# A low-rank update kernel: matrix A read by one transfer of 12 rows in place of three of 4 rows

## The chip, the cores and the metric

The kernel runs on one core of a Trainium2 chip. The metric is the device time of one execution in microseconds (us); lower is better. The core has five engines with an instruction stream each: TensorE (PE in the profile; PEld is its weight load), VectorE (DVE), ScalarE (ACT), GpSimd (POOL) and SyncE (SP). Here SP computes nothing: it only issues transfers, and all of the kernel's transfers go through its one queue. 16 DMA engines carry them out. Engines and transfers are kept in order by semaphores, which the kernel sets and waits for by hand.

## The reference

```python
batch, seq, d_model, r = 16, 512, 768, 16
x: (16, 512, 768) float32, A: (768, 16) float32, B: (16, 768) float32, scale = 0.5
lora = np.matmul(np.matmul(x, A), B)
return (x + scale * lora).astype(np.float32)
```

x has 8192 tokens of 768 values, 25.2 MB in and as much out. A and B are 48 KB each. To every token a correction of rank 16 is added.

## The kernel before, in words

**Tiling.** The tokens are cut into five parts (`PARTS = [9, 7, 16, 16, 16]`, in units of 128 tokens). Inside a part, each of the 128 partitions holds that many consecutive tokens, so a transfer's row in one partition is one long contiguous piece. All of x stays in on-chip memory (`x_sb`), in float32; the last part takes the place of the first two, once these are stored. A unit of 128 tokens is called a tile here; 64 tiles are worked on in 8 groups of 8.

**One group.** ScalarE and GpSimd cast four tiles each to float16 (`narrowed`, line 194, into `xn`). VectorE transposes them in 32 x 32 blocks (`turned`, line 250, into `xt`). TensorE multiplies the transposed tokens with a block-diagonal arrangement of A (`projected`, line 281, weights `w_bd`, result `y_ps`). ScalarE scales the 16 values per token and spreads them on the diagonal blocks of `y_bd` (line 238). TensorE multiplies these with B (`raised`, line 302, weights `y_bd`, moving `b_mm`, result in `lora_ps`). VectorE adds the result to x in place (`summed`, line 255). The store sends x back.

**The transfers, all on SP** (`on_sync`). In this order: load 0 (2 tiles) and load 1 (7 tiles) of x; then SP waits until `a_rows` is cleared and issues the three transfers of A (line 156); it waits until `b_rows` is cleared and issues B (line 160); then loads 2 to 5 (7, 8, 8 and 16 tiles). From there on each issue waits for something: stores 0 and 1 for the additions of the first two groups, load 6 for store 0 to land, load 7 for store 1, stores 2 to 4 for the sums of their parts (store 2 also for the start of the sixth group's product with B). Line 139 issues a load, line 149 a store.

**How A gets into its place.** A is seen as 12 blocks of 64 of its rows (`blocks`, 12 rows of 1024 values, 4 KB each). The first 32 partitions of `a_rows` are cleared by GpSimd (line 199). Transfer c (0, 1, 2) puts blocks 4c to 4c+3 into partitions c, c+4, c+8 and c+12. Each of the three adds 16 to the semaphore `s_a` when it has landed; GpSimd's first cast of x adds 1 to the same semaphore. VectorE waits until it is 49 and then transposes the 32 partitions of `a_rows` into `a_t` (line 243). GpSimd copies the 12 valid columns to float16 in block order (`w_one`, line 214), and then four times into the diagonal places of `w_bd` (line 220), which TensorE needs for its first projection.

**How B gets into its place.** Its 16 rows go into every fourth partition of `b_rows`; GpSimd casts them (line 212), TensorE spreads them over all partitions with a selecting matrix (line 315), and ScalarE copies the result to `b_mm` (line 231).

The order of the start on the other engines: GpSimd clears five tiles (lines 199 to 203), casts the first two tiles of x, casts B, then builds `w_one` and `w_bd`. ScalarE casts the other six tiles of the first group. VectorE transposes A first, then the first group's casts in two halves.

Of the kernel before, what the change touches and what calls it, by code (L numbers as in the profile page):

```python
# [18 lines left out]
SUB = 4  # L19

APART = 4
SETS, SET = 3, 4


@with_exitstack
def kernel(
# [11 lines left out]
    Q = 32  # L41
# [6 lines left out]
    NC = D // 64  # L48
# [6 lines left out]
    def sb(name, shape, dtype):  # L55
        return nc.alloc_sbuf_tensor(name, shape, dtype).ap()
# [10 lines left out]
    a_rows = sb("a_rows", [P, 64 * R], fp32)  # L67
    a_t = sb("a_t", [P, 2, R, Q], fp32)
    w_one = sb("w_one", [Q, NC, 2, R], MM_DT)
# [13 lines left out]
    def sem(name):  # L83
        sems.append(nc.alloc_semaphore(name))
        return sems[-1]
# [10 lines left out]
    def memory(t2, i, s, n):  # L96
        S = PARTS[i]
        return t2[ds(parts[i], S * P), :].rearrange("(p s) d -> p s d", s=S)[:, ds(s, n), :]

    def held(i, s, n):  # L100
        return tiles(where.index((i, s)), n)

    def tiles(t, n):
        return x_all[:, ds(t % ROOM, n), :]
# [7 lines left out]
        i, s = where[t]  # L112
        return next(k for k, ld in enumerate(LOADS) if ld[0] == i and ld[1] <= s < ld[1] + ld[2])

    assert SETS * SET == NC
    s_a, s_b = sem("s_a"), sem("s_b")
    s_ready, s_brows, s_pick = sem("s_ready"), sem("s_brows"), sem("s_pick")
    s_w, s_bh, s_bp, s_bm = sem("s_w"), sem("s_bh"), sem("s_bp"), sem("s_bm")
# [17 lines left out]
    def on_sync(e):  # L136
        def load(k):
            ld = LOADS[k]
            e.dma_start(out=held(*ld), in_=memory(x2, *ld)).then_inc(s_load[k], 16)  # L139

        def summed(k):
            e.wait_ge(s_sum, sorted(set(STORED)).index(STORED[k]) + 1)
            if STORED[k] + 1 < NG:

                e.sem_inc(s_free[PAIRS - 1], 1)

        def store(k, done):
            st = STORES[k]
            e.dma_start(out=memory(out2, *st), in_=held(*st)).then_inc(done, 16)

        load(0)
        load(1)
        e.wait_ge(s_ready, 1)
        blocks = A.rearrange("(c e) r -> c (e r)", e=64)
        for c in range(SETS):
            e.dma_start(
                out=a_rows[c : SET * SET : SET, :], in_=blocks[ds(c * SET, SET), :]
            ).then_inc(s_a, 16)
        e.wait_ge(s_brows, 1)
        e.dma_start(out=b_rows[0 : R * APART : APART, :], in_=B).then_inc(s_b, 16)  # L160
        for k in range(2, len(LOADS) - 2):
            load(k)

        for p in range(2, PAIRS):
            e.sem_inc(s_free[p], 1)
        summed(0)


        e.wait_ge(s_lora, 2 * PAIRS + 2)
        store(0, s_out0)  # L170
        store(1, s_out1)
        e.wait_ge(s_out0, 16)
        load(len(LOADS) - 2)
        e.wait_ge(s_out1, 16)
        load(len(LOADS) - 1)
        for k in range(2, len(STORES)):
            summed(k)
            if k == 2:


                e.wait_ge(s_raise, 6)
            store(k, s_out)
# [3 lines left out]
    def narrowed(e, copy, g, first, n=SUB):  # L186
        t = g * GROUP + first
        for k in dict.fromkeys(load_of(t + k) for k in range(n)):
            if (e, k) not in here:
                here.add((e, k))  # L190
                e.wait_ge(s_load[k], 16)
        if g:
            e.wait_ge(s_taken, g)
        ins = copy(out=xn[:, ds(first, n), :], in_=tiles(t, n))  # L194

        ins.then_inc(s_narrow if g else s_first if first else s_a, 1)

    def on_gpsimd(e):
        e.memset(a_rows[0:Q], 0.0).then_inc(s_ready, 1)  # L199
        e.memset(b_rows, 0.0).then_inc(s_brows, 1)  # L200
        e.memset(pick, 0.0).then_inc(s_pick, 1)
        e.memset(w_bd.rearrange("p c k m -> p (c k m)").bitcast(fp32), 0.0)  # L202
        e.memset(y_bd.rearrange("p s m -> p (s m)").bitcast(fp32), 0.0).then_inc(s_ready, 1)  # L203
        e.wait_ge(s_pick, 1)
        e.affine_select(  # L205
            out=pick, in_=pick, compare_op=mybir.AluOpType.not_equal, fill=1.0, base=0,
            pattern=[[0, NQ], [-APART, Q]], channel_multiplier=1,
        ).then_inc(s_pick, 1)
        narrowed(e, e.tensor_copy, 0, 0, SUB // 2)
        e.wait_ge(s_pick, 2)  # L210
        e.wait_ge(s_b, 16)
        e.tensor_copy(out=b_half, in_=b_rows).then_inc(s_bh, 1)  # L212
        e.wait_ge(s_ready, 3)
        e.tensor_copy(  # L214
            out=w_one.rearrange("i (c e) k r -> i c e (k r)", c=SETS),
            in_=a_t[0:Q].rearrange("i k r (e c) -> i c e (k r)", c=SET)[:, 0:SETS, 0:SET, :],
        ).then_inc(s_w, 1)
        e.wait_ge(s_w, 1)
        for b in range(NQ):
            e.tensor_copy(  # L220
                out=w_bd[ds(b * Q, Q), :, :, ds(b * Q, R)], in_=w_one
            ).then_inc(s_w, 1)
            e.wait_ge(s_w, b + 2)
        for g in range(1, NG):
            narrowed(e, e.tensor_copy, g, SUB)
# [13 lines left out]
            last.then_inc(s_spread, 1)  # L239

    def on_vector(e):
        e.wait_ge(s_a, SETS * 16 + 1)
        e.transpose(  # L243
            out=a_t[0:Q].rearrange("i k r c -> i (k r) c"),
            in_=a_rows[0:Q].rearrange("c (i k r) -> c (k r) i", k=2, r=R),
        ).then_inc(s_ready, 1)

        def turned(first, n):
            ts = [v[:, ds(first, n), :].bitcast(fp32) for v in (xt, xn)]
            return e.transpose(out=ts[0], in_=ts[1])  # L250

        def summed(g, p):
            xs = tiles(g * GROUP + 2 * p, 2)
            e.wait_ge(s_lora, g * PAIRS + p + 1)
            ins = e.tensor_tensor(out=xs, in0=xs, in1=lora[p % 2], op=mybir.AluOpType.add)  # L255
            if p + 1 == PAIRS and g in STORED:
                ins.then_inc(s_sum, 1)
            elif g + 1 < NG or p + 2 < PAIRS:
                ins.then_inc(s_free[p], 1)

        for h in range(2):
            e.wait_ge(s_first, h + 1)
            ins = turned(h * SUB, SUB)
        ins.then_inc(s_turned, 1)
        for g in range(NG):
            if g + 1 < NG:
                e.wait_ge(s_y, g + 1)
                e.wait_ge(s_narrow, 2 * (g + 1))  # L268
                turned(0, GROUP).then_inc(s_turned, 1)
            for p in range(PAIRS):  # L270
                summed(g, p)

    def on_tensor(e):
# [58 lines left out]
        for p in range(PAIRS):  # L332
            raised(p)

    on_sync(nc.sync)
    on_gpsimd(nc.gpsimd)
    on_scalar(nc.scalar)
    on_vector(nc.vector)
    on_tensor(nc.tensor)

# [43 lines left out]
```

## Time and profile before

| what | before |
|---|---|
| time, median of 3 runs | 123.47 us (123.41 to 123.53) |
| time of the profiled execution | 123.43 us |
| its span (first to last instruction) | 121.6 us |
| bytes moved in the span, mean rate | 50.43 MB, 415 GB/s |
| busy time VectorE | 81.7 us (67%) |
| busy time TensorE, its weight load | 49.8 us (41%), 29.2 us (24%) |
| busy time ScalarE, GpSimd | 37.4 us (31%), 28.4 us (23%) |
| three issues of A on SP | 0.58 to 0.76 us each |

The span is what the profiler sees between the first and the last instruction; the measured time has a little more on both sides of it. Times inside the profile count from the start of the span. A timeline line gives start and duration in us, the engine, the source line, the operation, what is written from what is read with the shapes, how often, and in brackets how long the engine sat idle before it and what ended that. SPq is SP's own queue of issues: its durations are those of issuing, not of the transfer.

The trace also has a record of every DMA packet: when it started, how long it took and how many bytes it moved. A packet here is one partition's row of a transfer, or a write of 4 bytes that counts up a semaphore.

### The profile page before, as it was taken

The page shows a single profiled execution, that of the slowest core. Times are in us where ns is not written, and L with a number is a line of the kernel's source. Part 1 is how long each engine was busy: PE and PEld are TensorE (multiplying, and loading weights), DVE is VectorE, ACT ScalarE, POOL GpSimd, SP SyncE. Part 2 cuts the span into 40 slices and gives each one's busy share as a digit, 9 for nine tenths or more (in the row PEclk, how much of TensorE's full clock was granted, in tenths as well). Part 3 has the DMA queues.
Part 4 walks back from the last instruction along what each step waited for, and adds up shares of the span by engine and source line. Part 5 has one row for each costly group of instructions (what it writes and reads, how often), then busy time and mean ns, then how long its engine had stood idle before and what let it go on. Part 6 is the DMA issues. An engine that isn't in the chain of part 4 may idle for free.

```text
span 121.6 us, 884 instructions
## 1 busy us (share of the span) xinstructions
PE 49.8 (41%) x322; PEld 29.2 (24%) x322; DVE 81.7 (67%) x42; ACT 37.4 (31%) x43; POOL 28.4 (23%) x24
## 2 busy tenths in 40 slices
PE   0000209487457547746745734774674320000000
PEld 0000006253223424424423322442442110000000
DVE  0000970599999999999999989999995990000000
ACT  4000967626408312735340093643004000000000
POOL 7730567126009002605300080620000000000000
PEclk9999999999999999999999999999999995555555
DMA  3999999999999897999999999998999899899890
GB/s 63 437 431 457 446 398 469 404 420 469 437 517 420 356 517 336 427 421 410 446 416 436 428 428 485 420 517 372 404 517 404 372 517 404 372 517 404 372 517 0
DMA packets 1928, 50.43 MB, mean 415 GB/s; under 512 B 236, under 2 KB 236, under 8 KB 392
## 3 DMA queue, kind: packets, MB, share of 16 engines
q1 hardware_dynamic: 1928, 50.43, 97.0%
HBM read 25.26 MB, written 25.17 MB: 415 GB/s over the span
## 4 chain that ended last, share of the span: by engine, by line
DVE 33%; DMA 29%; PE 9%; ACT 6%; POOL 2%; issue 2%; SPq 0%; DVEq 0%
DVE x_sb L255 21%; DMA x_sb<-in_x_dram 20%; DVE xt L250 12%; DMA out_dram<-x_sb 9%; PE ps_yt L281 6%; ACT xn L194 3%; PE lora_ps L302 3%; ACT y_bd L238 2%; POOL xn L194 2%; SPq L139 0%; SPq L379 0%; DVEq L268 0%; SPq L134 0%
## 5 line engine op out<-in xcount | busy, mean ns | idle before, releaser
L255 DVE TENSOR_TENSOR x_sb<-x_sb,lora_ps 128x1536 f32<-128x1536 f32 x32 | 53.7, 1735 | 1.4 <-PE lora_ps L302 1.4
L194 ACT CAST xn<-x_sb 128x3072 f16<-128x3072 f32 (+1 forms) x9 | 23.4, 2609 | 35.9 <-DMA x_sb<-in_x_dram 24.8
L302 PE MATMUL lora_ps<-b_mm,y_bd 128*128 128x512 f16 (+1 forms) x128 | 25.0, 328 | 22.6 <-ACT y_bd L238 14.3
L194 POOL CAST xn<-x_sb 128x3072 f16<-128x3072 f32 (+1 forms) x8 | 20.7, 2586 | 43.9 <-DMA x_sb<-in_x_dram 24.6
L250 DVE STREAM_TRANSPOSE xt<-xn 128x3072 f32<-128x3072 f32 (+1 forms) x9 | 27.1, 3006 | 5.3 <-PE ps_yt L281 4.4
L281 PE MATMUL ps_yt<-xt,w_bd 128*128 128x256 f16 x192 | 25.2, 282 | 12.2 <-DVE xt L250 12.2
L281 PEld LDWEIGHTS ps_yt<-xt,w_bd 128*128 128x128 f16 x192 | 18.5, 99 | 19.7 <-issue 15.4
L302 PEld LDWEIGHTS lora_ps<-b_mm,y_bd 128*128 128x128 f16 x128 | 10.6, 97 | 35.5 <-ACT y_bd L238 16.6
L238 ACT ACTIVATE y_bd<-ps_yt 32x256 f16<-32x256 f32 x32 | 12.0, 374 | 18.7 <-PE ps_yt L281 18.4
L243 DVE STREAM_TRANSPOSE a_t<-a_rows 32x1024 f32<-32x1024 f32 x1 | 2.0, 1955 | 12.2 <-DMA a_rows<-in_A_dram 12.2
L315 PE MATMUL lora_ps<-b_half,pick 128*128 128x512 f16 (+1 forms) x2 | 0.8, 500 | 13.5 <-POOL b_half L212 13.5
L315 PEld LDWEIGHTS lora_ps<-b_half,pick 128*128 128x128 f16 x2 | 0.1, 105 | 13.5 <-issue 13.5
L212 POOL CAST b_half<-b_rows 128x768 f16<-128x768 f32 x1 | 0.8, 827 | 5.5 <-DMA b_rows<-in_B_dram 5.5
L220 POOL COPY w_bd<-w_one 32x384 f16<-32x384 f16 x4 | 2.0, 500 | 0.2
L194 ACT ACT_TABLE_LOAD x1 | 1.3, 1283 | 0.9 <-SPq L134 0.9
L202 POOL MEMSET w_bd<- 128x1536 f32 x1 | 1.4, 1372 | 0.0
L214 POOL CAST w_one<-a_t 32x384 f16<-32x384 f32 x1 | 0.9, 857 | 0.9 <-DVE a_t L243 0.9
L199 POOL MEMSET a_rows<- 32x1024 f32 x1 | 0.9, 941 | 0.5 <-SPq L134 0.5
L231 ACT CAST b_mm<-lora_ps 128x768 f16<-128x768 f32 x1 | 0.8, 798 | 0.0
L200 POOL MEMSET b_rows<- 128x768 f32 x1 | 0.7, 728 | 0.0
L203 POOL MEMSET y_bd<- 128x512 f32 x1 | 0.5, 514 | 0.0
L205 POOL TENSOR_SCALAR_AFFINE_SELECT pick<-pick 128x128 f16<-128x128 f16 x1 | 0.3, 298 | 0.0
(5 smaller groups left out, 0.6 us busy)
## 6 DMA issues: line engine op xcount, KB each, us to landing
out_dram<-x_sb SPq DMA_DIRECT2D x3, 6144.0 KB, 20.1
x_sb<-in_x_dram SPq DMA_DIRECT2D x4, 3072.0 KB, 17.6
x_sb<-in_x_dram SPq DMA_DIRECT2D x1, 6144.0 KB, 41.6
x_sb<-in_x_dram SPq DMA_DIRECT2D x2, 2688.0 KB, 12.4
out_dram<-x_sb SPq DMA_DIRECT2D x1, 3456.0 KB, 11.5
out_dram<-x_sb SPq DMA_DIRECT2D x1, 2688.0 KB, 17.7
x_sb<-in_x_dram SPq DMA_DIRECT2D x1, 768.0 KB, 4.5
a_rows<-in_A_dram SPq DMA_DIRECT2D x3, 16.0 KB
```

The lines of the kernel that those rows point to most:

```text
L194: ins = copy(out=xn[:, ds(first, n), :], in_=tiles(t, n))
L199: e.memset(a_rows[0:Q], 0.0).then_inc(s_ready, 1)
L202: e.memset(w_bd.rearrange("p c k m -> p (c k m)").bitcast(fp32), 0.0)
L214: e.tensor_copy(out=w_one.rearrange("i (c e) k r -> i c e (k r)", c=SETS), in_=a_t[0:Q].rearrange("i k r (e c) -> i c e (k r)", c=SET)[:, ...
L220: e.tensor_copy(out=w_bd[ds(b * Q, Q), :, :, ds(b * Q, R)], in_=w_one).then_inc(s_w, 1)
L238: last = e.mul(out=y_bd[q, :, q], in_=y_ps[q, :, :], mul=sc)
L243: e.transpose(out=a_t[0:Q].rearrange("i k r c -> i (k r) c"), in_=a_rows[0:Q].rearrange("c (i k r) -> c (k r) i", k=2, r=R),).then_inc(s_r ...
L250: return e.transpose(out=ts[0], in_=ts[1])
L255: ins = e.tensor_tensor(out=xs, in0=xs, in1=lora[p % 2], op=mybir.AluOpType.add)
L281: mm = e.matmul(y_ps, w_bd[:, c, k, :], xv[:, :, c, :, k], start=(m == 0), stop=(m == MMS - 1),)
L302: mms.append(e.matmul(t[:, k, ds(n0, w)], y_bd[:, 2 * p + k, :], b_mm[:, ds(n0, w)], start=True, stop=True,))
L315: last = e.matmul(lora[0][:, 0, ds(n0, w)], pick.rearrange("p b r -> p (b r)"), b_half[:, ds(n0, w)], start=True, stop=True,)
```

## The change

The three transfers of A become one. Its 12 blocks go into partitions 0, 2, 4, ... 22 of `a_rows`, in order. The wait on VectorE is for 17 in place of 49. The copy that makes `w_one` takes the columns of `a_t` 2 apart in their own order, where it took them in three sets of four. Nothing else differs.

```diff
 APART = 4
-SETS, SET = 3, 4
+STEP = 2
...
-    assert SETS * SET == NC
+    assert STEP * NC <= Q
...
         blocks = A.rearrange("(c e) r -> c (e r)", e=64)
-        for c in range(SETS):
-            e.dma_start(
-                out=a_rows[c : SET * SET : SET, :], in_=blocks[ds(c * SET, SET), :]
-            ).then_inc(s_a, 16)
+        e.dma_start(out=a_rows[0 : STEP * NC : STEP, :], in_=blocks).then_inc(s_a, 16)
         e.wait_ge(s_brows, 1)
...
         e.tensor_copy(
-            out=w_one.rearrange("i (c e) k r -> i c e (k r)", c=SETS),
-            in_=a_t[0:Q].rearrange("i k r (e c) -> i c e (k r)", c=SET)[:, 0:SETS, 0:SET, :],
+            out=w_one.rearrange("i c k r -> i c (k r)"),
+            in_=a_t[0:Q].rearrange("i k r (c s) -> i s c (k r)", s=STEP)[:, 0, 0:NC, :],
         ).then_inc(s_w, 1)
...
     def on_vector(e):
-        e.wait_ge(s_a, SETS * 16 + 1)
+        e.wait_ge(s_a, 16 + 1)
```

## The prediction

> **What bounds the kernel now.** First the page, its table of 40 slices and its DMA parts:
>
> ```profile
> span 121.6 us, 884 instructions
> ...
> DMA  3999999999999897999999999998999899899890
> ...
> DMA packets 1928, 50.43 MB, mean 415 GB/s; under 512 B 236, under 2 KB 236, under 8 KB 392
> ...
> q1 hardware_dynamic: 1928, 50.43, 97.0%
> ```
>
> One queue carries 50.43 MB, and its packets fill 97% of the 16 DMA engines' span. No compute engine comes near that (VectorE 67%). The dips in the DMA row prove nothing: half-microsecond windows show shares up to 2.51, so a packet's time is booked near where it starts.
>
> So I went to the packet records of the trace (start, duration and size of each). A packet that starts within a few ns of another's end is its successor on the same engine; joined so, the 1928 packets fall into 16 chains (one join is by elimination, at 50.7 us), one per DMA engine. From 5.6 us on no chain has a gap over 6 ns: **no DMA engine is ever idle**, whatever the compute engines do. Each chain carries the same x rows and result rows (one packet per partition row: 799 ns for 21504 bytes, 1815 ns for 49152) and one row of B (121 ns); four chains carry three rows of A each (159 ns a row). The chains end with store 4. The start of each one's last packet, the 4-byte semaphore write, in us:
>
> ```
> four with A:     119.74  119.86  119.98  119.99
> twelve without:  119.20  119.36  119.40  119.41  119.41  119.47
>                  119.55  119.57  119.62  119.85  120.01  120.22
> ```
>
> The end is the **last** chain's, at 120.23, and it has no A row. The page's store row answers to it: issue at 100.64 plus 20.1 us gives a landing at 120.7.
>
> ```profile
> out_dram<-x_sb SPq DMA_DIRECT2D x3, 6144.0 KB, 20.1
> ```
>
> The profiled execution's 123.43 us is therefore 1.98 (first packet) + 118.25 (last chain) + 0.47 (to the landing, 120.70) + 0.91 (end of the span) + 1.82 outside the span. The median of the three runs shown is 123.47, 0.04 above.
>
> The page's chain of waits ends in the last additions on VectorE (100.6 us) and leaves out the 20 us of store 4, so I don't read the bound from it.
>
> **The change, part by part.** The queue's issues in order of time (start, duration, engine, line):
>
> ```profile
> 0.97 0.85 SPq L139 DMA_DIRECT2D x_sb<-in_x_dram  x2
> 1.92 2.02 SPq L156 DMA_DIRECT2D a_rows<-in_A_dram  x3
> 3.98 0.54 SPq L160 DMA_DIRECT2D b_rows<-in_B_dram  x1
> 4.57 2.08 SPq L139 DMA_DIRECT2D x_sb<-in_x_dram  x4
> 44.45 0.82 SPq L149 DMA_DIRECT2D out_dram<-x_sb  x2
> ```
>
> 1. *Issue on SP.* Three issues (2.02 us) become one. No issue of 12 rows is shown; the rows around it are 0.54 (B, 16 rows) and 0.58 to 0.76 (4 rows), and I take 0.7. B's issue then waits for the memset of b_rows (ends 1.84 + 0.73 = 2.57) and starts near 2.65; loads 2 to 5 are issued from about 3.2 instead of 4.57. Their first packets run at 10.8 us and later, behind loads 0 and 1 in each chain, so 1.3 us of earlier issue is worth 0: the queue is not dry. If that cover were gone it would be worth up to 1.3 us.
>
> 2. *The DMA engines.* The page counts 236 packets under 512 bytes. Those are the chains' 4-byte writes: 14 transfers (8 loads, 5 stores, B) x 16, and 12 for the three of A, so each 4-row transfer ran on 4 engines, always the same four. B's 16 rows ran on 16. I take it that 12 rows run on 12 engines, one each, the old four among them. An A row with its 4-byte write moves its chain by 161 ns (A packets start 161 ns apart). So the old four lose two rows, **-0.32 us** each; eight others gain one, **+0.16**; four stay. The bytes are the same. The last chain is one of the twelve without A: by mere count it is one of the eight in 2 cases of 3. Then its end goes from 120.23 to 120.39. If it is one of the other four, its end stays, and the next (120.01 + 0.16 = 120.17) stays below it.
>
> [...]
>
> 3. *When A arrives.* VectorE waits for A until 12.23; load 1 lets ScalarE start at 12.12.
>
> ```profile
> 12.12 4.13 ACT L194 CAST xn<-x_sb 128x1536 f16<-128x1536 f32 x2 [9.93 <-DMA x_sb<-in_x_dram]
> 12.23 1.96 DVE L243 STREAM_TRANSPOSE a_t<-a_rows 32x1024 f32<-32x1024 f32 x1 [12.23 <-DMA a_rows<-in_A_dram]
> ...
> 14.12 1.72 DVE L250 STREAM_TRANSPOSE xt<-xn 128x1536 f32<-128x1536 f32 x1
> 14.25 0.86 POOL L214 CAST w_one<-a_t 32x384 f16<-32x384 f32 x1 [0.90 <-DVE a_t L243]
> 15.17 2.18 POOL L220 COPY w_bd<-w_one 32x384 f16<-32x384 f16 x4
> ...
> 16.28 1.78 DVE L250 STREAM_TRANSPOSE xt<-xn 128x1536 f32<-128x1536 f32 x1 [0.44 <-ACT xn L194]
> ...
> 18.21 4.26 PE L281 MATMUL ps_yt<-xt,w_bd 128*128 128x256 f16 x24 [3.92 <-DVE xt L250]
> ```
>
> A now waits for twelve engines in place of four, with less on each. Its rows sit ahead of B's in every chain, and B had landed when GpSimd read it at 12.52; B itself slips by at most one A row. So A comes between 11.6 (its first landing on an engine before) and about 12.7. Later by up to 0.44 us costs nothing: VectorE then idles that long for ScalarE's casts before 16.28. Beyond it there is more cover: a delay reaches the end only if store 0 comes too late. It is issued at 44.45, its packets can start about 1.0 us later (load 0: 0.97 to 1.98), and the earliest chain has load 5 until 46.47, so 1.0 us more. Taken at 0.
>
> 4. *The copy to w_one* reads rows 2 apart in place of 4 apart, 384 elements a partition as before. Bounds: 0.50 (a copy of 384 to w_bd) to 1.46 us (GpSimd's cast of 1536); I keep 0.86. The copies to w_bd end at 17.35 and TensorE waits for VectorE until 18.1, so +0.6 is still hidden. Transposes, memsets and the wait (17 in place of 49, one landing in place of three) cost the same.
>
> **Sum**: 123.43 + 0.16 = **123.60**, 0.1% above the median. 0.2% of it is 0.25 us, about what a measurement of this kernel can tell from no change, so this counts as the same.
>
> **Rivals.**
> - *The last chain gets no row*: 123.43. For it: 1 case in 3 by the count. Against: the count.
> - *Relief of the four A chains* (faster). From 50 us on the last chain's packets run 1.0 us over the usual durations, 0.69 of it after 62 us, where no other chain has more than 0.08; the chain at 120.01 got there by one packet of 1.60 us in place of 0.80. If timed executions lack both, the A chains (120.00) set the end. They drop by 0.32, and the next (119.85, late from the start) holds the end at -0.14 or, with a row, at +0.02. Only without that one too does the whole -0.32 come near: 123.1 to 123.4. Against: the runs lie within 0.12 us of each other and 0.04 from the profiled one.
> - *A stall in the ramp* (slower). B and loads 2 to 5 would be issued from 2.65 us on, while load 0's packets run (1.98 to 5.1). There packets already stall: between 3 and 6 us four chains have 0.15, 0.18, 0.38 and 0.53 us over the usual 234 ns. What is lost there is never regained, as no chain idles. If such a stall falls on the last chain together with its row, it is 123.43 + 0.16 + 0.15 to 0.53 = 123.75 to 124.1. It decides from 0.1 us of stall on the last chain, 0.15 on the next. Against: few chains are hit, and the three issues of A fall into the same stretch before.
> - *The change doesn't spread the rows*: with three on four engines as before, no change; with twelve on one engine, 12 x 0.161 = 1.93 us on one chain: 119.2 to 120.2 plus 1.93 gives 124.3 to 125.4. Against: engines equal rows in both cases shown.
> - *Fewer issues pay for themselves*: 1.3 us off, 122.1, if loads 2 to 5 were late now. Against: the chains without gaps. [...]
>
> **How the numbers follow.** Last chain takes a row, 0.42; it takes none, 0.22; relief, 0.15, of which 0.08 is over 0.2%; stall, 0.16; no spread, 0.03; fewer issues pay, 0.02. Faster 0.08 + 0.02 = 0.10, slower 0.16 + 0.03 = 0.19, same 0.71. The range 123.2 to 123.9 leaves out half of the relief, the larger half of the stalls, and the last two: about 0.2.
>
> **What the changed profile would show.** One issue of about 0.7 us at 1.92, B near 2.65, four loads from 3.2; again 236 packets under 512 bytes and 1928 in all; twelve chains with one A row. VectorE's first transpose between 11.7 and 12.7, TensorE's first projection still after ScalarE's casts at 18.2, store 0 near 44.45. The four old chains should no longer be among the late ones. I am wrong if a chain idles between 6 and 119 us, if A's rows run on fewer engines, or if the end moves by more than 0.25 us with a last chain that has none of the causes above.

## The result, and the profile after

The changed kernel is **slower**: 124.26 us, the median of 7 runs (123.89 to 124.77), beside 123.56 us for the kernel before in the same series (7 runs, 123.41 to 123.74). The ratio is 1.0056, interval 1.0034 to 1.0079: +0.70 us where the prediction had +0.16, above the range of 123.2 to 123.9. The runs also lie further apart, by 0.88 us against 0.33 us. The profiled execution of the changed kernel took 123.89 us, the lowest of its seven; that of the kernel before took 123.43.

From the page of the changed kernel, the lines that answer to those shown of the kernel before:

```profile
span 122.1 us, 882 instructions
...
DMA  3999999999997996999999989799799699699790
...
DMA packets 1928, 50.43 MB, mean 413 GB/s; under 512 B 236, under 2 KB 236, under 8 KB 392
...
q1 hardware_dynamic: 1928, 50.43, 96.7%
...
out_dram<-x_sb SPq DMA_DIRECT2D x3, 6144.0 KB, 20.4
x_sb<-in_x_dram SPq DMA_DIRECT2D x4, 3072.0 KB, 18.0
```

The same 1928 packets carry the same bytes. Loads of 3072 KB now take 18.0 us from issue to landing (17.6 before), and the stores 20.4 (20.1). SP's issues, with the columns as before:

```profile
1.92 0.90 SPq L153 DMA_DIRECT2D a_rows<-in_A_dram  x1
2.87 0.55 SPq L155 DMA_DIRECT2D b_rows<-in_B_dram  x1
3.46 2.01 SPq L137 DMA_DIRECT2D x_sb<-in_x_dram  x4
44.42 0.82 SPq L147 DMA_DIRECT2D out_dram<-x_sb  x2
```

The loads are issued 1.1 us earlier, and store 0 at the same time as before (44.45). The start of the compute chain did not move either (start, duration, engine, line; the brackets say what ended the idle time):

```profile
12.10 1.96 DVE L238 STREAM_TRANSPOSE a_t<-a_rows 32x1024 f32<-32x1024 f32 x1 [12.10 <-DMA a_rows<-in_A_dram]
...
14.12 0.85 POOL L209 CAST w_one<-a_t 32x384 f16<-32x384 f32 x1 [0.73 <-DVE a_t L238]
...
18.20 4.24 PE L276 MATMUL ps_yt<-xt,w_bd 128*128 128x256 f16 x24 [3.87 <-DVE xt L245]
```

What did move is the first packets of load 2, which run where A and B have just passed. The stretch from 10.5 to 13 us, first of the kernel before, then of the changed one (stretch, length, busy time and count by engine, granted clock, DMA share, GB/s):

```profile
10.50:13.00 2.50, 0.00 (x0) 0.00 (x0) 0.77 (x1) 0.88 (x1) 0.48 (x1) 1.00 0.99 418
```

```profile
10.50:13.00 2.50, 0.00 (x0) 0.00 (x0) 0.90 (x1) 0.89 (x1) 0.44 (x1) 1.00 0.93 366
```

The last column falls from 418 to 366 GB/s. Joined into chains as in the prediction, the packets say why: behind B's row, the first x row of 21504 bytes takes 0.91 to 0.96 us (0.95 in most chains) in place of 0.799, in **all 16 chains**, those with a row of A and those without. Summed over the packets that start from 10.5 to 13 us, a chain is 0.15 to 0.25 us over the usual durations (median 0.16; at most 0.02 in the kernel before). I call this the shared stall. The last chain's last packet starts at 120.68, 0.46 later than before: 0.16 for a row of A, 0.25 for its part of the stall, 0.05 elsewhere. One chain, not the one that ends last, idles once in this execution, for 0.18 us near 64.2 us.

### The profile page after: what moved, and what is told of

Its sections match the earlier page's. It is cut to its first block, busy times and chain, and to the rows that moved or that the text cites. A ratio compares the mean times of both kernels' runs of the same rounds, so it can differ in the third digit from the quotient of the medians.

```text
span 122.1 us, 882 instructions
## 1 busy us (share of the span) xinstructions
PE 49.8 (41%) x322; PEld 29.2 (24%) x322; DVE 81.7 (67%) x42; ACT 37.5 (31%) x43; POOL 28.4 (23%) x24
## 2 busy tenths in 40 slices
DMA packets 1928, 50.43 MB, mean 413 GB/s; under 512 B 236, under 2 KB 236, under 8 KB 392
## 3 DMA queue, kind: packets, MB, share of 16 engines
q1 hardware_dynamic: 1928, 50.43, 96.7%
## 4 chain that ended last, share of the span: by engine, by line
DVE 33%; DMA 30%; PE 9%; ACT 6%; POOL 2%; issue 2%; SPq 0%; DVEq 0%
DVE x_sb L250 21%; DMA x_sb<-in_x_dram 20%; DVE xt L245 12%; DMA out_dram<-x_sb 10%; PE ps_yt L276 6%; ACT xn L189 3%; PE lora_ps L297 3%; ACT y_bd L233 2%; POOL xn L189 2%; SPq L137 0%; SPq L374 0%; DVEq L263 0%; SPq L132 0%
## 5 line engine op out<-in xcount | busy, mean ns | idle before, releaser
L297 PEld LDWEIGHTS lora_ps<-b_mm,y_bd 128*128 128x128 f16 x128 | 10.5, 98 | 35.6 <-ACT y_bd L233 16.7
## 6 DMA issues: line engine op xcount, KB each, us to landing
out_dram<-x_sb SPq DMA_DIRECT2D x3, 6144.0 KB, 20.4
```

The lines of the kernel that those rows point to most:

```text
L297: mms.append(e.matmul(t[:, k, ds(n0, w)], y_bd[:, 2 * p + k, :], b_mm[:, ds(n0, w)], start=True, stop=True,))
```

## The experiments

Each is an edit of the kernel before or of the changed one, and each ratio is to the kernel before measured beside it. A diff shows the lines that matter; where the number of transfers changes, VectorE's wait for A changes with it. "Stall" is the median over the chains of the excess from 10.5 to 13 us; "rows" is how many rows of A the last chain carries, as far as the joins can tell (chains that tie can swap). Every run has one profile, so a stall is that of one execution.

The theory was **placement**: what a row of A costs depends on where in `a_rows` it lands, through the shared stall. Its rivals were **timing** (B and the loads are issued earlier and collide with something: the prediction's stall in the ramp) and the **copy** (the new reading order of `w_one` delays the compute chain).

**The changed kernel again**, unaltered.

> The changed kernel once more, unaltered, for a second profile and more times. Its first profile (123.89) has the last chain 0.46 us later than before: one A row is 0.16, a stall of 0.16 us that all 16 chains show near 12 us is most of the rest; but its median is 124.26, 0.37 above that profile. ROW theory (A's row on the last chain, the rest accident): the stall near 12 us is gone, the last chain again holds an A row, time 123.6 to 123.9. TIMING theory (B and loads 2 to 5 are issued 1.1 us earlier, and that stalls the engines): the stall or another one common to many chains is there again, 123.9 to 124.8.

124.50 us, ratio 1.0064 (1.0044 to 1.0085). Stall 0.26, one row. The effect repeats. This profile shows a part that the first did not, told at the late starts below.

**Hold B and the loads back** to their old place in time:

```diff
         e.wait_ge(s_brows, 1)
+        e.wait_ge(s_hold, 1)
         e.dma_start(out=b_rows[0 : R * APART : APART, :], in_=B).then_inc(s_b, 16)
...
-        e.memset(w_bd.rearrange("p c k m -> p (c k m)").bitcast(fp32), 0.0)
+        e.memset(w_bd.rearrange("p c k m -> p (c k m)").bitcast(fp32), 0.0).then_inc(s_hold, 1)
```

> The changed kernel, but SP waits before B's issue until GpSimd has cleared w_bd (near 4.0 us), so that B and loads 2 to 5 are issued when they were before. ROW theory: as the changed kernel, 123.6 to 124.3. TIMING theory: as before or with the row alone, 123.4 to 123.7.

124.35 us, ratio 1.006 (1.0046 to 1.0075), stall 0.20. SP's issues of this kernel show that the edit did its work:

```profile
1.92 0.89 SPq L153 DMA_DIRECT2D a_rows<-in_A_dram  x1
4.13 0.55 SPq L156 DMA_DIRECT2D b_rows<-in_B_dram  x1
4.72 2.04 SPq L137 DMA_DIRECT2D x_sb<-in_x_dram  x4
```

B and the loads go out 0.15 us later than in the kernel before, and neither the stall nor the time goes away. Timing falls.

**The new copy alone**, in the kernel before (A's blocks are then taken in a wrong order, one in four a cleared row; the work of the engines is the same):

```diff
-            out=w_one.rearrange("i (c e) k r -> i c e (k r)", c=SETS),
-            in_=a_t[0:Q].rearrange("i k r (e c) -> i c e (k r)", c=SET)[:, 0:SETS, 0:SET, :],
+            out=w_one.rearrange("i c k r -> i c (k r)"),
+            in_=a_t[0:Q].rearrange("i k r (c s) -> i s c (k r)", s=2)[:, 0, 0:NC, :],
```

> The kernel before with one line of the change: GpSimd's copy to w_one reads the columns 2 apart, as in the changed kernel, while A still lands 4 apart (so the blocks are taken in a wrong order and one in four is a cleared row: A is not what is multiplied). PLACEMENT theory (the partitions A is written to cost the time): as before, 123.4 to 123.8, no stall at 12 us. COPY theory: 124.0 to 124.6.

123.55 us, ratio 0.9991 (0.9978 to 1.0004), stall 0. The copy falls. Beside it, the kernel before unaltered:

> The kernel before, unaltered, as a control with a profile of its own. All five profiles with A's rows 2 partitions apart show a stall of 0.11 to 0.31 us that the 16 chains of packets share near 12 us; the one profile of before has none. If the stall belongs to the placement of the rows it is absent here; if it comes and goes by chance it may be here too. Time 123.4 to 123.8 either way.

123.72 us, ratio 1.001 (0.9998 to 1.0022), stall 0. So a ratio within about 0.1%, some 0.1 us, is nothing. The four further profiles of this kernel below have none either (0 to 0.014 us).

**Other numbers of transfers into the new places** (partitions 0, 2, ... 22):

```diff
-        e.dma_start(out=a_rows[0 : STEP * NC : STEP, :], in_=blocks).then_inc(s_a, 16)
+        for c in range(3):
+            e.dma_start(
+                out=a_rows[c * STEP * 4 : (c + 1) * STEP * 4 : STEP, :], in_=blocks[ds(c * 4, 4), :]
+            ).then_inc(s_a, 16)
```

> A again by three transfers of 4 rows, but into the changed layout, partitions 0, 2, ... 22. ROW theory: three rows on each of the old four chains, time as before, 123.4 to 123.7. TIMING theory: issue times as before, so also 123.4 to 123.7. LAYOUT theory (rows 2 apart, or the copy to w_one, cost the time): 124 to 124.6.

124.17 us, ratio 1.0047 (1.002 to 1.0074), stall 0.135, no row on the last chain. Three issues on four engines, at the same times as in the kernel before, and most of the loss is still there: it does not need the rows to spread over twelve engines. From the kernel before this one differs only by the new places and the new copy, and the copy alone cost nothing. So the places by themselves cost 0.57 us of the 0.70, whatever the path by which they do it. With two transfers of six (the same edit with 6 for 4):

> A by two transfers of 6 rows, changed layout. By the counts seen so far each runs on 6 engines, two rows each, so six chains get +0.32 and ten none; B and loads 2 to 5 are issued about 0.5 us earlier than before. ROW theory: as before (123.4 to 123.7) if the chain that ends last has no A row, 123.75 to 124.0 if it has two. TIMING theory: in between, 123.7 to 124.2.

124.26 us, ratio 1.0055 (1.0038 to 1.0072), stall 0.11, two rows on the last chain.

**Which places?** Two kernels that put the same rows elsewhere. One transfer with rows 4 apart (partitions 0 to 44; VectorE reads only the first 32, so a third of A is left out and the rest is taken in a wrong order):

```diff
-        e.dma_start(out=a_rows[0 : STEP * NC : STEP, :], in_=blocks).then_inc(s_a, 16)
+        e.dma_start(out=a_rows[0 : 4 * NC : 4, :], in_=blocks).then_inc(s_a, 16)
```

> The changed kernel with its 12 rows 4 partitions apart (0 to 44) in place of 2. Only the first 32 partitions are read on, so a third of A is left out and the others are taken in a wrong order; the engines' work is the same. PLACEMENT theory: no stall at 12 us, 123.5 to 123.8. COUNT theory (one transfer of 12 rows, or 12 engines, costs the time whatever the partitions): stall there, 124.0 to 124.6.

124.10 us, ratio 1.0046 (1.0025 to 1.0066), stall 0.145. No stall was expected: rows 4 apart, as in the kernel before, don't make it go. And three transfers whose rows are 6 apart (0, 6, 12, 18, then from 2, then from 4):

```diff
-        e.dma_start(out=a_rows[0 : STEP * NC : STEP, :], in_=blocks).then_inc(s_a, 16)
+        for c in range(3):
+            e.dma_start(
+                out=a_rows[c * STEP : NC * STEP : 3 * STEP, :], in_=blocks[c:NC:3, :]
+            ).then_inc(s_a, 16)
```

> The changed placement (partitions 0, 2, ... 22), filled by three transfers of 4 rows that are 6 partitions apart (0, 6, 12, 18; then 2, 8, 14, 20; then 4, 10, 16, 22), as the kernel before interleaves its own. If what costs the time is two rows within one group of 4 partitions written at the same moment by one transfer, it is gone: 123.4 to 123.8. If the partitions alone decide (rows 2 apart, or rows beyond 15), 124.0 to 124.6 with a stall at 12 us.

123.81 us, ratio 1.0032 (1.0006 to 1.0058), stall 0.20, no row on the last chain.

Two readings were left. **High**: the stall comes from rows in higher partitions than the old 0 to 14. **Home**: the stall comes unless row n of a transfer lands in the n-th group of four partitions (row 0 in 0 to 3, row 1 in 4 to 7, ...); that is read from the placements alone. In the kernel before all twelve rows are at home (0, 4, 8, 12; 1, 5, 9, 13; ...); in the changed one only row 0 is (row 1 lands in partition 2, row 2 in 4). Four kernels on which the two disagree. Two have low partitions, most of them away from home (9 and 11 of the 12 rows), where home says a stall and high says none, by STEP = 1 in the changed kernel: three transfers (a loop as above) into 0 to 3, 4 to 7 and 8 to 11, and one into 0 to 11.

```diff
-STEP = 2
+STEP = 1
```

> A by three transfers of 4 rows into partitions 0 to 3, 4 to 7 and 8 to 11. HIGH theory (rows in partitions from 16 on bring the stall at 12 us): no stall, 123.4 to 123.8. [...]

123.97 us, ratio 1.0036 (1.0011 to 1.0061), stall 0.24. Five of its ten runs lie at 123.54 to 123.79 and five at 124.15 to 124.89; the profile is of the second kind, so whether the stall is in every run is not known.

> The changed kernel with its 12 rows in partitions 0 to 11. HIGH theory: no stall at 12 us, 123.5 to 123.9 (a row on the last chain, 0.16). HOME theory: stall, 124.0 to 124.6.

124.29 us, ratio 1.0068 (1.0044 to 1.0093), stall 0.44, the largest, where twelve rows crowd into three groups of four. Two have high partitions at home: two transfers of six rows, 4 apart (0 to 20, and 1 to 21), and one of eight (0 to 28) with one of four (1 to 13). In both, the copy to `w_one` is fitted to the new order; in the second it becomes two copies.

```diff
-SETS, SET = 3, 4
+SETS, SET = 2, 6
...
-                out=a_rows[c : SET * SET : SET, :], in_=blocks[ds(c * SET, SET), :]
+                out=a_rows[c : SET * 4 : 4, :], in_=blocks[ds(c * SET, SET), :]
```

> A by two transfers of 6 rows 4 apart: partitions 0, 4, ... 20 and 1, 5, ... 21. Six chains get two rows each. HIGH theory: 21 is beyond 15, stall at 12 us, 123.8 to 124.5. HOME theory: the n-th row is in the n-th group of four, no stall, 123.4 to 123.8. Against two_of_six (2 apart, stall 0.11, 124.26) only the distance differs.

123.92 us, ratio 1.0032 (1.0018 to 1.0046), stall 0, two rows on the last chain (the joins allow none as well). Against the two transfers of six above, the places and the copy that follows them are all that differs.

```diff
-        for c in range(SETS):
+        for c, n0, n in ((0, 0, 8), (1, 8, 4)):
             e.dma_start(
-                out=a_rows[c : SET * SET : SET, :], in_=blocks[ds(c * SET, SET), :]
+                out=a_rows[c : 4 * n : 4, :], in_=blocks[ds(n0, n), :]
```

> A by a transfer of 8 rows (partitions 0, 4, ... 28) and one of 4 (1, 5, 9, 13); the copy to w_one becomes two, which adds about 0.5 us of GpSimd behind 0.7 us of cover. HIGH theory: stall at 12 us, 123.8 to 124.5. HOME theory: no stall, 123.4 to 123.8, 0.16 more if the last chain is one of the eight.

123.77 us, ratio 1.0016 (1.0006 to 1.0026), stall 0.02, one row. The stretch from 10.5 to 13 us tells the extremes apart without any joining: first two of six at home, then one transfer into 0 to 11.

```profile
10.50:13.00 2.50, 0.00 (x0) 0.00 (x0) 0.80 (x1) 1.03 (x1) 0.48 (x1) 1.00 1.03 435
```

```profile
10.50:13.00 2.50, 0.00 (x0) 0.00 (x0) 0.46 (x1) 1.02 (x1) 0.17 (x1) 1.00 0.93 315
```

Over all these profiles it is 418 to 435 GB/s in the kernels without the stall and 315 to 401 in those with it. All four kernels come out as home says and against high, and home also fits the others that put rows 2 or 6 apart (three transfers 6 apart: only row 0 of the first two and row 1 of the first are at home). It does not fit the one transfer with rows 4 apart: there every row n is in the n-th group of four, and the stall was 0.145.

And B has rows 4 apart too: its first twelve go to partitions 0 to 44 of `b_rows`, and B goes with no stall in the kernel before. So home sorts all the kernels but the one transfer with rows 4 apart, and no trace shows which engine writes which partitions. The three placements of A without a stall also share rows 4 apart from the first group on and at most eight rows a transfer; no run separates home from that.

By rows alone at 0.161 us and the stall, against what was measured (us over the kernel before measured beside it):

```
                        rows   stall   sum    measured
kernel before again       0    0       0      +0.11
new copy alone            0    0       0      -0.06
8 + 4, at home            1    0.02    0.18   +0.18
2 x 6, at home            2    0       0.32   +0.33
3 x 4, 6 apart            0    0.20    0.20   +0.20
3 x 4, 0 to 11            0    0.24    0.24   +0.38
3 x 4, 2 apart            0    0.135   0.135  +0.57
1 x 12, 4 apart           1    0.145   0.31   +0.49
2 x 6, 2 apart            2    0.11    0.43   +0.66
changed kernel            1    0.16    0.32   +0.70
  again                   1    0.26    0.42   +0.90
  B and loads held        1    0.20    0.36   +0.75
1 x 12, 0 to 11           1    0.44    0.60   +0.70
```

Of the kernels without the stall, the two with rows at home match to 0.01 us, which is partly luck: the unaltered kernel came out at +0.11. Of those with it, one matches and the others go 0.1 to 0.5 over, and their runs lie wide apart (0.3 to 1.6 us, against 0.2 to 0.5). Something is added in some of their executions.

**Late starts.** What is added shows in the second profile of the changed kernel (124.50 us):

```profile
PEclk9999999999999999999999997699999965555555
```

```profile
18.20 5.28 PE L276 MATMUL ps_yt<-xt,w_bd 128*128 128x256 f16 x24 [3.84 <-DVE xt L245]
```

```profile
45.46 0.82 SPq L147 DMA_DIRECT2D out_dram<-x_sb  x2
56.05 7.48 SPq L137 DMA_DIRECT2D x_sb<-in_x_dram  x2
76.02 26.29 SPq L147 DMA_DIRECT2D out_dram<-x_sb  x3
```

All 24 products of the first projection took the slow 0.37 to 0.42 us each; in the first profile the last ten took 0.27 to 0.30. So the projection took 5.28 us and not 4.24, and store 0 left at 45.46, 1 us late. (The row of the granted clock doesn't show this start; it shows a dip near 75 us that the first profile's row lacks.) Near 62 us the chains together lose 11.7 us of packet time (1.3 in the first profile), and load 6 lands late:

```profile
71.01 2.75 ACT L189 CAST xn<-x_sb 128x3072 f16<-128x3072 f32 x1 [7.28 <-DMA x_sb<-in_x_dram]
```

That was 69.79 in the first profile. Store 2 leaves at 76.02 (74.58), and several chains run dry for 0.2 to 0.35 us near 76.5. The kernel with B held back (5.28 us as well) loses 10.2 us near 62, and its chains run dry for up to 0.2 us.

The start is late in some executions of either kernel. In the first profile of each, the trace's record of the granted clock, at full, starts only inside the first projection, at 21.24 us in the kernel before and at 21.17 in the changed one; ahead of it most products take 0.42 us, behind it 0.27. (The row above counts the time ahead of that record as full.) How many of the 24 products are slow varies from run to run: over the profiles they take 4.1 to 5.3 us together. Runs without a trace have only their mean granted clock. In the 18 profiles without added products, those with a mean under 0.895 are the seven whose first projection took 5.0 us or more, so that is the mark of a late start here. The kernel before takes 123.59 us with it (28 runs) and 123.60 without (54); the changed kernel 124.52 (6 runs, 124.02 to 124.77) and 124.08 (5 runs, 123.89 to 124.35). Over all runs of the nine lines of the table with a stall, those with a late start lie 0.75 us over the kernel before by their median (34 runs) and the others 0.37 (25); in the four lines without it, 0.12 (13) and 0.08 (22).

To take the late starts away, eight more products run on TensorE ahead of the first projection, in each kernel (called warmed below); they write a tile that is overwritten later:

```diff
+        for _ in range(8):
+            e.matmul(
+                lora[1][:, 0, ds(0, 512)], pick.rearrange("p b r -> p (b r)"),
+                b_half[:, ds(0, 512)], start=True, stop=True,
+            )
```

> The kernel before with eight needless products on TensorE (selecting matrix by B, 512 columns, into a bank that is overwritten later) between B's spreading at 14.3 us and the first projection at 18.2, so that the granted clock is full when the projection starts. The first projection should take some 2.7 us in every execution, in place of 4.3 or 5.3. If TensorE's start matters only where transfers are disturbed, the time is as before, 123.4 to 123.7.

124.13 us, ratio 1.0065. Expected was the time of the kernel before.

> The changed kernel with the same eight products. Theory: the row on the chain that ends last (0.16) and the shared stall (0.15 to 0.27) stay, and what the changed kernel loses beyond them (0.2 to 0.4 in its median, and its spread) comes from executions in which the first projection is slow and the additions come 1 us late. Then 123.85 to 124.05 with a spread under 0.4 us. Rival: the extra loss has nothing to do with the late start; 124.2 to 124.6, spread 0.5 or more.

124.32 us, ratio 1.008. The first projection of the warmed changed kernel (2.83 us in the warmed kernel before):

```profile
18.00 2.84 PE L276 MATMUL ps_yt<-xt,w_bd 128*128 128x256 f16 x24 [0.45 <-DVE xt L245]
```

By spans the theory holds, in four runs of each. The changed kernel's, 122.1 to 123.0 (median 122.4) without the products, are 122.0 to 122.1 with them; the kernel before has 121.6 to 121.9 with them (median 121.85), and 121.8 as its median without. The difference shrinks from 0.6 to 0.25 us. The stall is still there (0.24 in the changed kernel's profile, 0 in the other), and the row and the stall would be 0.40; in the warmed kernel before, though, the chain that ends last is one with three rows of A. By times the expectation missed: the time outside the span rose from 1.8 us to 2.0 to 2.45 in both kernels, which no run explains.

**Does a late start cost the kernel before nothing because its rows are at home?** Four more profiles of it, to catch one:

> The kernel before, unaltered, for a profile of an execution in which TensorE's clock rises late (it does in about 4 of 10). If late additions alone bring the second stall near 62 us, it is here too (over 5 us summed over the chains) and the last chain is hardly touched; if it takes the changed placement, it is below 3 us.

123.71 us.

> As before_third: another profile of the kernel before, for the same purpose.

123.52 us.

> The kernel before, unaltered, once more for a profile with a mean clock of 0.885 to 0.89 (the clock rises after the first projection, 23 us or later). If late additions alone bring the large stall near 62 us, its sum over the chains is about 10 us here; if it takes the changed placement too, under 5.

123.65 us.

> The kernel before, unaltered, for the same purpose as before_fifth: a large stall near 62 us (10 us over the chains) if a late clock alone brings it, under 5 us if the changed placement is needed.

123.59 us. Only the sixth caught a start as late as that of the second profile above (5.28 us; the others 4.87, 4.10 and 4.93):

```profile
17.97 5.28 PE L281 MATMUL ps_yt<-xt,w_bd 128*128 128x256 f16 x24 [3.80 <-DVE xt L250]
```

```profile
45.23 0.82 SPq L149 DMA_DIRECT2D out_dram<-x_sb  x2
55.86 7.02 SPq L139 DMA_DIRECT2D x_sb<-in_x_dram  x2
74.38 27.87 SPq L149 DMA_DIRECT2D out_dram<-x_sb  x3
```

Store 0 is nearly as late, but the chains lose 4.5 us near 62 instead of 11.7, store 2 leaves at 74.38, and no chain runs dry. But the kernel before is not free of such gaps. Its third and fifth profiles, with milder starts, lose 5.3 and 3.8 us near 62, and their store 2 leaves late too, at 75.22 and 75.18. In both, several chains run dry near 76 us, for up to 0.44 and 0.47 us, and the times are 123.71 and 123.65. By the bounds set beforehand (over 5 us near 62 if a late start alone brings the loss), the third speaks for that and the sixth against. Nor does every late start with the stall end badly: one transfer into 0 to 11, with the largest stall and a first projection of 5.03 us, loses 1.9 us near 62 and has no gap. So the loss near 62 and the gaps near 76 come in both placements; the times above say that the changed one pays more for a late start, and the path is not settled. No version tried beats the kernel before.

## Why the prediction was wrong

- **Failed: part 2, "The DMA engines".** It let a row of A move "its chain by 161 ns" and no other chain. The count of engines, the author's estimate from the transfers of 4 and 16 rows, and the row on the last chain hold: 236 packets under 512 bytes again, 12 chains with a row, the last one +0.16. But the prediction asked only which engine carries a row, not where the row lands. In the new places the rows go with a stall on every chain, 0.15 to 0.25 us here, 0.25 on the last chain. With the row, that takes the profiled execution, the fastest, to +0.46. Measured by itself, as three transfers into the new places, the term that was missing is worth +0.57 in the median (0.25 to 0.91 by its interval); with the row's 0.16 that is 0.73 for a measured 0.70, closer than the interval warrants. (The prediction's own sum, 123.43 + 0.16, is 123.59 and not 123.60; nothing hangs on it.)
- **Part 3, "Taken at 0"**, held for what it summed: A came at 12.10, as said, and nothing followed from that. What it left out is that the cover ahead of store 0, some 1.0 us, was read from one execution whose first projection took 4.26 us. Over the profiles it takes 4.1 to 5.3, and the latest store 0 is 1.0 us late. In the kernel before this costs nothing (123.59 against 123.60), in the changed kernel some 0.4 us (124.52 against 124.08).
- **"No DMA engine is ever idle"** was read from one execution as well. It is so in that profile, but in four of the other five profiles of the kernel before some chain idles near 62 or 76 us, for as long as 0.15 to 0.56 us. The line "I am wrong if a chain idles" came true for the changed kernel too, 0.18 us on one chain in the first profile and more in the second.
- **Part 1, issue on SP.** The issue took 0.90 us (I took 0.7, bounds 0.54 to 0.76), B 2.87 instead of 2.65, the loads 3.46 instead of 3.2. Worth 0, as said: holding them back changed nothing.
- **Part 4, the copy**: 0.85 us against 0.86, hidden. Right.
- **The rivals.** A stall in the ramp was the right kind at the wrong place and for the wrong reason: not from 2 to 5 us, but from 10.5 to 13, on all chains, and not through earlier issue. Relief was worth nothing: which chains are the old four can't be told any more, but all chains with a row except the last end by 119.96 (last packet), and the end is at 120.68.

Open: why a row in the wrong place slows all 16 chains, and why one transfer of A's twelve rows 4 apart goes with a stall of 0.145 us when B's sixteen, 4 apart as well, go with none in the kernel before; what the loss near 62 us is, and why late starts cost more with the changed placement; why three transfers 2 apart exceed their sum by 0.4 us. That the placement costs most of the +0.70 is shown, and so is the stall that comes with it; that late starts are the rest is a comparison of runs, and no run sets the stall and the late start apart.

## What to carry to other kernels

Where the DMA engines hardly idle, as here, a transfer's cost is what it does to every engine's chain (0.16 us on its chain for a row of A, and 0.11 to 0.44 us on all 16 in places away from home): ask which engine takes each row and which partitions it writes. What worked for A's rows here was row n of a transfer in the n-th group of four partitions, with at most eight rows a transfer (stall 0 to 0.02 us), even at the price of more issues; one transfer of twelve rows 4 apart did not (0.145 us). A cover of 1 us that is read from one execution is not a cover if a step ahead of it varies by 1 us from run to run; profile the kernel before more than once, and read the spread. When a change moves a kernel by half a per cent, look at the spread of its runs as well as their median: here the wider spread was a large part of the effect.

## What the runs showed of the hardware that was not expected

- Twelve rows of 4 KB, 48 KB of 50.43 MB, slow the next packets of all 16 chains by 0.11 to 0.44 us or by 0 to 0.02, depending on the partitions they go to: with two transfers of six, 0.11 us with rows 2 apart and 0 with rows 4 apart.
- SP's issue time depends on whether the partitions are adjacent: 0.90 us for 12 rows 2 or 4 apart and 0.39 for 12 adjacent ones; for 4 rows 0.58 to 0.76 us when 2, 4 or 6 apart and 0.25 to 0.35 when adjacent.
- Eight more products on TensorE, ahead of everything that sets the end, lengthened not the span but the time outside it, from 1.8 to as much as 2.45 us.
